# A hybrid attention and RWKV-7 block on one core: the place of VectorE's low parts in the attention stage, and three weight loads that wait for TensorE

## The chip, the core and the metric

The kernel runs on one core of one Trainium2 chip. The metric is device time in microseconds (us), the median of the timed runs. Time of the kernel before: 856.06 us, median of 3 runs (855.99 to 856.78).

## What is computed

One decoder block on 512 tokens of width 1024, all in float32:

```
h = rms_norm(x, attn_norm_g)
u = h @ w_in                                  # 1024 -> 1536 attention + 1792 RWKV + 2048 gates
o_sb = stick_breaking_attention(q, k, v)      # 8 heads of 64, causal
o_rw = rwkv7_time_mix(u_rw, ...)              # 8 heads of 64, a recurrence over the tokens
merged = g_sb * (o_sb @ w_up_sb) + g_rw * (o_rw @ w_up_rw)
x = x + merged @ w_out
x = x + square(relu(rms_norm(x) @ w_ff1)) @ w_ff2
x = x + sigmoid(rms_norm(x) @ w_ple_gate) * (p @ w_ple_proj)
return rms_norm(x, final_norm_g)
```

In stick-breaking attention a weight is `exp(log_sigmoid(z) + reversed running sum of log_sigmoid(-z))` over the scores `z` of a causal row. The change touches the order of the work in the attention stage and in the RWKV stage alone.

## The kernel before, in words

**Split products.** A float32 product is done as three products of rounded parts: both operands are split into a high part (a rounded copy in the format fp32r, made by ScalarE) and a low part (the rest, a subtraction on VectorE). TensorE multiplies high by high, low by high and high by low. For weights this is `mm3` (L244 to L246): w_hi with the high and low parts of the activations, then w_lo. The low part of an operand is thus used last, and always comes out of VectorE.

**Weights.** They come as 512 KB units in the order of the list `seq`. A unit's life is: `load_to` issues the load of `w_raw` on SyncE's queue (L182; four buffers), ScalarE casts it to `w_hi` (L225), VectorE subtracts to get `w_lo` (L227), TensorE uses both. `fetch_to` traces cast and subtraction a few units ahead (`AHEAD = 3`) of the unit that is used. Units are named by kind and number: U_QKV (attention's queries, keys and values), U_RW (RWKV's inputs), U_GSB and U_GRW (the two gates), U_UPSB (attention's up-projection).

**Attention** (about 22 to 145 us). The 8 heads go in pairs (`hp` 0 to 3). While head n is worked on, TensorE's stream is filled with the projections of the next pair and with the first RWKV projections; the function `drive` interleaves generators step by step. For each head there are three blocks. `scores` makes z (L511, L512, into `ps_z`), ScalarE and VectorE make from it `sp` (L519) and split it into `sph` and `spl` (L274, L275). `attend` multiplies `sph` and `spl` by a triangular matrix for the running sums (L558, L562), ScalarE takes the exponential into `sp`, VectorE rounds it to `wh` (L564) and subtracts to get `wl` (L565), and TensorE multiplies `wh` and `wl` by the values into `ps_o` (L550). This line of work, scores to ps_o, is called the chain below. Beside it `projected` splits the next pair's queries (qT, L447, into `qq` and on VectorE `ql`, L455) and keys (kT, L459, into `kk`, whose low half VectorE writes at L463).

**RWKV** (about 150 to 400 us). For each pair `prepare` builds the recurrence's small matrices, `scan` runs the recurrence of the pair before, and `filling` puts gate and up-projections between their steps. In `prepare` the inverse of small triangular matrices is built from 32x32 products: L877 (64 of them to a group), L937 (32), L945 (32); then 64x64 products (L956, 32). The gates' results are written to DRAM by SyncE (L739) and read again later (L725).

**What sets the order.** Each engine runs its own queue in order. A scheduler puts the traced instructions in place on each engine. `tc.issue_after(x)` around an instruction makes it stand behind x on x's engine; it is an order of issue alone and waits for nothing else. `tc.add_manual_dep(a, b, Sync)` makes a really wait until b is done, also across engines.

Of the kernel before, what the change touches and what calls it, by code (L numbers as in the profile page):

```python
# [14 lines left out]
ALU = mybir.AluOpType  # L15
# [78 lines left out]
def tile_block(ctx: ExitStack, tc: tile.TileContext, xT, xt, pT, wts, lora, cols_d, gfin_d, consts_d, out, dbg=None):  # L94
# [65 lines left out]
    ready, loaded, sums12 = {}, [], {}  # L160
    state = {"i": 0, "used": 0, "due": 0}
    AHEAD = 3
    homes = {}
    sources = {}
    sP4 = {}
# [10 lines left out]
    def load_to(n):  # L176
        while len(loaded) < min(n, len(seq)):
            i = len(loaded)
            loaded.append(None)
            if seq[i] not in sources and seq[i][0] not in (U_S3, U_S4):  # L180
                loaded[i] = wpool.tile([P, 1024], F32, name="w_raw", bufs=4)
                sync.dma_start(out=loaded[i], in_=unit(i))  # L182
                if seq[i][0] == U_FF2 and seq[i][2] == 3:
                    pool.dma_start(out=loaded[i], in_=wts[UBASE[U_FF2] + seq[i][1] * 8 + 4 + seq[i][3]], accum_op=ALU.add)

# [10 lines left out]
    def made(i):  # L196
# [10 lines left out]
            return sums12.pop(seq[i][1:])[:, 2]  # L207
        return loaded[i]

    def fetch_to(n, ahead=0):  # L210
        while state["i"] < min(n, len(seq)):
            i = state["i"]
            state["i"] += 1
            load_to(i + 1 + ahead)
            raw = made(i)
            if seq[i] in homes:
                hi, lo = homes[seq[i]]()
            elif seq[i][0] == U_S4:
                hi = wpool.tile([P, 512], F32R, name="w_hi4", bufs=1)
                lo = wpool.tile([P, 512], F32R, name="w_lo4", bufs=1)  # L220
            else:
                hi = wpool.tile([P, 1024], F32R, name="w_hi")
                lo = wpool.tile([P, 1024], F32R, name="w_lo")
            with tc.issue_after(state["hx"] if seq[i] == (U_FF1, 4) else state["fourth"][0]) if seq[i] in ((U_FF1, 4), (U_OUT, 2), (U_OUT, 3)) else nullcontext():
                state["cast"] = act.copy(out=hi, in_=raw).ins  # L225
            with tc.issue_after(state["fourth"][1]) if seq[i] in homes and seq[i][0] == U_OUT else nullcontext():
                state["wlo"] = dve.tensor_tensor(out=lo, in0=raw, in1=r32(hi), op=ALU.subtract).ins  # L227
            if seq[i] == (U_OUT, "s", 4):
                state["fourth"] = state["cast"], state["wlo"]
            ready.setdefault(seq[i], []).append((hi, lo))  # L230
# [99 lines left out]
    with ExitStack() as sA:  # L330
# [43 lines left out]
        with ExitStack() as s1:  # L374
# [68 lines left out]
            def projected(hp, i, ps):  # L443

                if i == 0:
                    t = p1.tile([P, T], F32, name="qT", tag="qkv", bufs=3)
                    dve.scalar_tensor_tensor(out=t, in0=ps, scalar=0.125, in1=rs, op0=ALU.mult, op1=ALU.mult)  # L447

                    qq = [p1.tile([P, T], F32R, name=f"qq{hh}") for hh in range(2)]

                    ql = qls[hp % 2]
                    for hh, (sl, ot) in enumerate((HALVES, HALVES[::-1])):
                        act.copy(out=qq[hh][sl], in_=t[sl])
                        pool.tensor_copy(out=qq[hh][ot], in_=t[sl])
                        dve.tensor_tensor(out=ql[hh][sl], in0=t[sl], in1=r32(qq[hh][sl]), op=ALU.subtract)  # L455
                    heads[hp] = [qq, ql]
                elif i == 1:
                    t = p1.tile([P, T], F32, name="kT", tag="qkv", bufs=3)
                    dve.tensor_tensor(out=t, in0=ps, in1=rs, op=ALU.mult)  # L459
                    kk = [p1.tile([P, T], F32R, name=f"kk{hh}") for hh in range(2)]  # L460
                    for hh, (sl, ot) in enumerate((HALVES, HALVES[::-1])):
                        act.copy(out=kk[hh][sl], in_=t[sl])
                        dve.tensor_tensor(out=kk[hh][ot], in0=t[sl], in1=r32(kk[hh][sl]), op=ALU.subtract)  # L463
                    heads[hp].append(kk)
                else:
                    t = p1.tile([P, T], F32, name="vT", tag="qkv", bufs=3)
                    dve.tensor_tensor(out=t, in0=ps, in1=rs, op=ALU.mult)
                    late.append([3, hp, t])
# [29 lines left out]
            def scores(hp, hh, got):  # L498

                qq, ql, kk = heads[hp][:3]  # L500
                sp = p1.tile([P, 1280], F32, name="sp")
                sph = p1.tile([P, 1280], F32R, name="sph")
                spl = p1.tile([P, 1280], F32R, name="spl")
                zt = {}
                got.update(zt=zt, sp=sp, sph=sph, spl=spl)
                for b, js in BLOCKS:
                    zt[b] = ps_z()

                    for j in js:
                        s = slice(j * P, (j + 1) * P)  # L510
                        pe.matmul(z(zt, j), kk[hh][:, s], qq[hh][:, j * P:T], start=j < 3, stop=False, skip_group_check=True)  # L511
                        pe.matmul(z(zt, j), kk[hh][:, s], ql[hh][:, j * P:T], start=False, stop=False, skip_group_check=True)  # L512
                        pe.matmul(z(zt, j, 0, P), ident_b, caus_b, start=False, stop=True, skip_group_check=True)
                    s, n = BANKS[b]
                    e = sp[:, s:s + n]
                    act.activation(out=e, in_=zt[b][:, :n], func=AF.Abs)
                    act.activation(out=e, in_=e, func=AF.Exp, scale=-1.0)
                    act.activation(out=e, in_=e, func=AF.Ln, bias=1.0)
                    dve.scalar_tensor_tensor(out=e, in0=zt[b][:, :n], scalar=0.0, in1=e, op0=ALU.max, op1=ALU.add)  # L519
                    split(sph[:, s:s + n], spl[:, s:s + n], e)  # L520
                    if b == 1:

                        sums = p1.tile([P, 512], F32, name="sums", bufs=1)
                        hi, lo = (p1.tile([P, 640], F32R, name=name) for name in ("sums_hi", "sums_lo"))
                        for to, i in ((0, 2), (256, 1)):
                            for part, d in ((sph, hi), (spl, lo)):
                                pool.tensor_copy(out=d[:, to:to + P], in_=part[:, ZB[i]:ZB[i] + P])
                        dve.tensor_tensor(out=sums[:, 0:P], in0=sp[:, ZB[2] + P:ZB[2] + 2 * P], in1=sp[:, ZB[3]:ZB[3] + P], op=ALU.add)
                        split(hi[:, P:2 * P], lo[:, P:2 * P], sums[:, 0:P])
                        for c, other in ((0, sp[:, ZB[2]:ZB[2] + P]), (P, sums[:, 0:P])):  # L530
                            dve.tensor_tensor(out=sums[:, 256 + c:384 + c], in0=sp[:, ZB[1] + P + c:ZB[1] + 2 * P + c], in1=other, op=ALU.add)
                        pool.tensor_copy(out=hi[:, 384:640], in_=sums[:, 256:512])
                        pool.tensor_tensor(out=lo[:, 384:640], in0=sums[:, 256:512], in1=r32(hi[:, 384:640]), op=ALU.subtract)
                        got["later"] = hi, lo
                    yield

            def attend(hp, hh, got):
# [17 lines left out]
                for b, js in BLOCKS:  # L555
                    s, n = BANKS[b]
                    for part in (sph, spl):
                        pe.matmul(zt[b][:, :n], tri, part[:, s:s + n], start=False, stop=False, skip_group_check=True)  # L558
                    j = js[0]
                    for part, later in zip((sph, spl), got["later"]):  # L560
                        after = (later[:, 256:640], later[:, 0:256], part[:, ZB[3]:ZB[3] + P])[j]
                        pe.matmul(z(zt, j, P), neg, after, start=False, stop=part is spl, skip_group_check=True)  # L562
                    state["exp"] = act.activation(out=sp[:, s:s + n], in_=zt[b][:, :n], func=AF.Exp)
                    dve.tensor_copy(out=wh[:, s:s + n], in_=sp[:, s:s + n])  # L564
                    dve.tensor_tensor(out=wl[:, s:s + n], in0=sp[:, s:s + n], in1=r32(wh[:, s:s + n]), op=ALU.subtract)  # L565
                    yield
                    output(before)
                    before = js
# [68 lines left out]
        with ExitStack() as s2:  # L637
# [108 lines left out]
            def prepare(hp, got):  # L746
# [187 lines left out]
                ps3 = ps[:, 0:256].rearrange("p (k x) -> p k x", k=8)  # L934
                for k in range(8):
                    for r in (0, 2):
                        pe.matmul(ps3[QUADS[r + 1], k], LM[QUADS[r], k, r // 2, 32:64], X[QUADS[r], k, :], start=True, stop=True)  # L937
                for r in (0, 2):
                    act.copy(out=Yc[QUADS[r + 1]], in_=ps3[QUADS[r + 1]])
                yield  # L940
# [748 lines left out]
```

## Time and profile before

| | |
|---|---|
| median of 3 timed runs | 856.06 us (855.99 to 856.78) |
| the profiled execution | 859.3 us, of it the span 857.5 us and 1.8 us around it |
| mean granted clock of TensorE | 0.996 |
| chain that ended last, by engine | PE 87%, DVE 9%, issue 1%, ACT 1%, DMA 1% |
| DMA over the span | 145 GB/s, 124.23 MB |

PE is TensorE, DVE VectorE, ACT ScalarE, POOL GpSimd, SP SyncE; SPq is SyncE's issuing. A row of the timeline gives start and duration in us, engine, line, operation, result <- operands, tile shape, count, and in brackets the idle time ahead of it with what ended it; "issue" there means that no other engine's work is seen to end the wait. Matmuls are pipelined, so where one instruction waited the spacing of the starts says more than the idle figure. A row of windows gives for a stretch its length, then for PE, PEld (TensorE's weight loads), DVE, ACT and POOL the busy time and number of instructions, then the clock granted to TensorE, the DMA engines' busy share and GB/s. A row of waits gives the total, the count and the longest. A row of the DMA queues gives packets, MB and the share of 16 engines' time.

### The profile page before, as it was taken

How to read it: one execution, taken by the hardware profiler on the slowest of the kernel's cores; microseconds unless marked ns; L12 is line 12 of the kernel's file. 1: busy time of each engine (PE TensorE's matmuls, PEld its weight loads, DVE VectorE, ACT ScalarE, POOL GpSimd, SP SyncE). 2: the span in 40 equal slices, each digit the busy share in tenths (PEclk: the TensorE clock that was granted, in tenths of full speed). 3: DMA queues.
4: the chain of work that ended last, by engine and by line, in shares of the span. 5: the costliest groups of instructions: out<-in, count | busy, mean ns of one | idle time of the engine just before them, and what ended most of it. 6: DMA issues, size and time to landing. Idle time of an engine off the chain costs nothing.

```text
span 857.5 us, 14647 instructions
## 1 busy us (share of the span) xinstructions
PE 840.8 (98%) x5594; PEld 697.5 (81%) x5594; DVE 712.6 (83%) x1264; ACT 513.1 (60%) x804; POOL 105.5 (12%) x174
## 2 busy tenths in 40 slices
PE   8999999999999999999999999999999999999996
PEld 5778788777777777777888888899889989988885
DVE  7989987896987969867896597899879988997767
ACT  7878887734436243533585575458647844783843
POOL 1332432001212101020000101000110010010000
PEclk9999999999999999999999999999999999999999
DMA  8311213421220323427882676973985489275402
GB/s 320 101 50 62 87 62 135 123 96 54 63 88 25 103 83 115 162 97 232 284 258 95 189 228 156 232 202 102 227 234 150 139 240 241 96 221 145 174 23 99
DMA packets 40197, 124.23 MB, mean 145 GB/s; under 512 B 4544, under 2 KB 4544, under 8 KB 40128
## 3 DMA queue, kind: packets, MB, share of 16 engines
q1 hardware_dynamic: 34944, 104.42, 35.7%
q0 software_dynamic: 5184, 18.88, 12.1%
q8 instruction: 44, 0.72, 0.4%
q14 instruction: 25, 0.20, 0.1%
HBM read 108.08 MB, written 10.49 MB: 138 GB/s over the span
## 4 chain that ended last, share of the span: by engine, by line
PE 87%; DVE 9%; issue 1%; ACT 1%; DMA 1%; SPq 0%; DVEq 0%; ACTq 0%
PE ps_m L244 14%; PE ps_m L245 14%; PE ps_m L246 14%; PE ps_m L260 9%; PE ps_m L259 9%; PE ps_m L261 9%; PE ps_g L877 1%; DVE w_lo L227 1%; PE ps_o L550 1%; PE ps_s L1005 1%; PE ps_z L558 1%; PE ps_c L996 1%; PE ps_g L967 1%; DVE LX L899 1%; DVE own L888 1%
## 5 line engine op out<-in xcount | busy, mean ns | idle before, releaser
L225 ACT CAST w_hi<-w_raw 128x1024 fp32r<-128x1024 f32 x122 | 128.0, 1051 | 122.4 <-PE ps_m L245 77.4
L227 DVE TENSOR_TENSOR w_lo<-w_raw,w_hi 128x1024 fp32r<-128x1024 f32 x122 | 149.0, 1224 | 24.2 <-ACT w_hi L225 23.5
L244 PE MATMUL ps_m<-h_hi,w_hi 128*128 128x512 f32 x320 | 130.6, 410 | 0.8 <-ACT w_hi L274 0.7
L246 PE MATMUL ps_m<-h_hi,w_lo 128*128 128x512 f32 x320 | 128.6, 402 | 0.0
L245 PE MATMUL ps_m<-h_lo,w_hi 128*128 128x512 f32 x320 | 128.2, 401 | 0.3 <-DVE h_lo L407 0.3
L244 PEld LDWEIGHTS ps_m<-h_hi,w_hi 128*128 128x128 f32 x320 | 60.7, 190 | 12.6 <-ACT w_hi L274 1.1
L246 PEld LDWEIGHTS ps_m<-h_hi,w_lo 128*128 128x128 f32 x320 | 60.4, 189 | 12.0
L245 PEld LDWEIGHTS ps_m<-h_lo,w_hi 128*128 128x128 f32 x320 | 60.5, 189 | 11.3 <-DVE h_lo L407 1.3
L245 PE MATMUL ps_m<-hx,w_hi 128*128 128x256 f32 (+1 forms) x208 | 65.8, 316 | 0.0
L244 PE MATMUL ps_m<-hx,w_hi 128*128 128x256 f32 (+1 forms) x208 | 65.8, 316 | 0.0
L246 PE MATMUL ps_m<-hx,w_lo 128*128 128x256 f32 (+1 forms) x208 | 65.7, 316 | 0.0
L244 PE MATMUL ps_m<-tb,w_hi 128*128 128x256 f32 x192 | 54.3, 283 | 0.0
L245 PE MATMUL ps_m<-tb,w_hi 128*128 128x256 f32 x192 | 54.3, 283 | 0.0
L246 PE MATMUL ps_m<-tb,w_lo 128*128 128x256 f32 x192 | 54.3, 283 | 0.0
L259 PE MATMUL ps_m<-w_hi,fS 128*128 128x512 f32 x128 | 49.8, 389 | 0.0
L260 PE MATMUL ps_m<-w_lo,fS 128*128 128x512 f32 x128 | 49.8, 389 | 0.0
L261 PE MATMUL ps_m<-w_hi,fS 128*128 128x512 f32 x128 | 49.8, 389 | 0.0
L245 PEld LDWEIGHTS ps_m<-hx,w_hi 128*128 128x128 f32 x208 | 39.6, 191 | 3.0 <-DVE hx L1158 0.4
L244 PEld LDWEIGHTS ps_m<-hx,w_hi 128*128 128x128 f32 x208 | 39.6, 191 | 2.8 <-ACT hx L1157 0.2
L246 PEld LDWEIGHTS ps_m<-hx,w_lo 128*128 128x128 f32 x208 | 39.6, 191 | 2.5
L259 PE MATMUL ps_m<-w_hi,fA 128*128 128x512 f32 x96 | 37.4, 389 | 0.0
L260 PE MATMUL ps_m<-w_lo,fA 128*128 128x512 f32 x96 | 37.4, 389 | 0.0
(425 smaller groups left out, 2147.2 us busy)
## 6 DMA issues: line engine op xcount, KB each, us to landing
w_raw<-in_wts_dram SPq DMA_DIRECT2D x129, 512.0 KB, 4.0
gates<-gg SPq DMA_DIRECT2D x16, 256.0 KB, 2.0
w_raw<-in_wts_dram POOLq DMA_DIRECT2D x8, 512.0 KB, 6.6
x_in<-in_xT_dram SPq DMA_DIRECT2D x8, 256.0 KB, 5.5
gb<-gates SPq DMA_DIRECT2D x8, 256.0 KB, 4.5
tmp<-gates SPq DMA_DIRECT2D x8, 256.0 KB, 2.9
upsb<-tmp SPq DMA_DIRECT2D x8, 256.0 KB, 5.1
ga<-upsb SPq DMA_DIRECT2D x8, 256.0 KB, 6.2
```

Source lines behind the costliest of these rows:

```text
L225: state["cast"] = act.copy(out=hi, in_=raw).ins
L227: state["wlo"] = dve.tensor_tensor(out=lo, in0=raw, in1=r32(hi), op=ALU.subtract).ins
L244: pe.matmul(ps, wh, xh[:, k, t], start=first, stop=False, skip_group_check=skip)
L245: pe.matmul(ps, wh, xl[:, k, t], start=False, stop=False, skip_group_check=skip)
L246: pe.matmul(ps, wl, xh[:, k, t], start=False, stop=last, skip_group_check=skip)
L259: pe.matmul(ps, xh[:, k + j], wh, start=first and j == 0, stop=False, skip_group_check=True)
L260: pe.matmul(ps, xh[:, k + j], wl, start=False, stop=False, skip_group_check=True)
L261: state["row"] = pe.matmul(ps, xl[:, k + j], wh, start=False, stop=last and j == 1, skip_group_check=True).ins
L550: pe.matmul(ps_o[:, j * P:T], vv[:, j, hh, :, :].rearrange("p a d -> p (a d)"), part[:, ZB[j]:ZB[j] + ZN[j]], start=j == 2 and part is wh, ...
L558: pe.matmul(zt[b][:, :n], tri, part[:, s:s + n], start=False, stop=False, skip_group_check=True)
L877: last = pe.matmul(ps[rows, k], left[rows, k, :], rhs[rows, k], start=True, stop=True)
L888: dve.tensor_tensor(out=own8[rows], in0=own, in1=b8[rows].broadcast_to([32, 8, 32]), op=ALU.mult)
```

## The change

It has two parts.

**Attention: low parts behind the chain's.** A variable `state["urgent"]` holds VectorE's latest low part of the chain: the last `spl` that `scores` traced or the last `wl` that `attend` traced. The subtractions for `w_lo` of the U_QKV and U_RW units, for `ql` and for `kk` are traced inside `behind()`, so each of them stands on VectorE behind the chain's latest low part.

**RWKV: three raw loads wait.** The loads of U_GRW units 5 and 6 and of U_UPSB unit 3 wait for the last matmul of the group L937 in `prepare` of pair 2 (both gate units) and of pair 3 (the up-projection unit).

```diff
+    LATER = {(U_GRW, 5): 2, (U_GRW, 6): 2, (U_UPSB, 3): 3}
...
-                sync.dma_start(out=loaded[i], in_=unit(i))
+                load_ = sync.dma_start(out=loaded[i], in_=unit(i))
+                if seq[i] in LATER:
+                    tc.add_manual_dep(load_.ins, state["lm", LATER[seq[i]]].name,
+                                      mybir.DependencyInfo(mybir.DependencyClass.Sync, mybir.DependencyReason.DATA), reason="order")
...
+    def behind():
+        return tc.issue_after(state["urgent"]) if "urgent" in state else nullcontext()
...
-            with tc.issue_after(state["fourth"][1]) if seq[i] in homes and seq[i][0] == U_OUT else nullcontext():
+            with tc.issue_after(state["fourth"][1]) if seq[i] in homes and seq[i][0] == U_OUT else behind() if seq[i][0] in (U_QKV, U_RW) else nullcontext():
                 state["wlo"] = dve.tensor_tensor(out=lo, in0=raw, in1=r32(hi), op=ALU.subtract).ins
...
-                        dve.tensor_tensor(out=ql[hh][sl], in0=t[sl], in1=r32(qq[hh][sl]), op=ALU.subtract)
+                        with behind():
+                            dve.tensor_tensor(out=ql[hh][sl], in0=t[sl], in1=r32(qq[hh][sl]), op=ALU.subtract)
...
-                        dve.tensor_tensor(out=kk[hh][ot], in0=t[sl], in1=r32(kk[hh][sl]), op=ALU.subtract)
+                        with behind():
+                            dve.tensor_tensor(out=kk[hh][ot], in0=t[sl], in1=r32(kk[hh][sl]), op=ALU.subtract)
...
                     split(sph[:, s:s + n], spl[:, s:s + n], e)
+                    state["urgent"] = state["lo"]
...
-                    dve.tensor_tensor(out=wl[:, s:s + n], in0=sp[:, s:s + n], in1=r32(wh[:, s:s + n]), op=ALU.subtract)
+                    state["urgent"] = dve.tensor_tensor(out=wl[:, s:s + n], in0=sp[:, s:s + n], in1=r32(wh[:, s:s + n]), op=ALU.subtract).ins
...
-                        pe.matmul(ps3[QUADS[r + 1], k], LM[QUADS[r], k, r // 2, 32:64], X[QUADS[r], k, :], start=True, stop=True)
+                        state["lm", hp] = pe.matmul(ps3[QUADS[r + 1], k], LM[QUADS[r], k, r // 2, 32:64], X[QUADS[r], k, :],
+                                                    start=True, stop=True).ins
```

The kernel's lines move by 7 to 11 (L227 is L234 after, L455 is L463, L463 is L472, L182 is L183, L739 is L749).

Of the order on VectorE, the place where pair 3's queries are split, before (sp, spl, wh, wl belong to the chain):

```order
L227 TENSOR_TENSOR w_lo<-w_raw,w_hi 128x1024
L275 TENSOR_TENSOR spl<-sp,sph 128x512
L564 CAST wh<-sp 128x256
L455 TENSOR_TENSOR ql_196<-qT,qq_1010 64x512
L565 TENSOR_TENSOR wl<-sp,wh 128x256
L455 TENSOR_TENSOR ql_197<-qT,qq_1011 64x512
```

And after:

```order
L234 TENSOR_TENSOR w_lo<-w_raw,w_hi 128x1024
L582 TENSOR_TENSOR oo<-ps_o,oo 64x512
L528 SCALAR_TENSOR_TENSOR sp<-ps_z,sp 128x512
L454 SCALAR_TENSOR_TENSOR qT<-ps_m,rs 128x512
L282 TENSOR_TENSOR spl<-sp,sph 128x512
L574 CAST wh<-sp 128x256
L575 TENSOR_TENSOR wl<-sp,wh 128x256
L463 TENSOR_TENSOR ql_196<-qT,qq_1010 64x512
L463 TENSOR_TENSOR ql_197<-qT,qq_1011 64x512
```

w_lo has moved up ahead of oo, sp and qT; both ql stand behind wl.

Still on VectorE, the place where pair 3's keys are split, before:

```order
L459 TENSOR_TENSOR kT<-ps_m,rs 128x512
L227 TENSOR_TENSOR w_lo<-w_raw,w_hi 128x1024
L463 TENSOR_TENSOR kk_1121<-kT,kk_1121 64x512
L463 TENSOR_TENSOR kk_1122<-kT,kk_1122 64x512
L519 SCALAR_TENSOR_TENSOR sp<-ps_z,sp 128x512
L572 TENSOR_TENSOR oo<-ps_o,oo 64x512
L564 CAST wh<-sp 128x256
L275 TENSOR_TENSOR spl<-sp,sph 128x512
L565 TENSOR_TENSOR wl<-sp,wh 128x256
```

And after:

```order
L467 TENSOR_TENSOR kT<-ps_m,rs 128x512
L528 SCALAR_TENSOR_TENSOR sp<-ps_z,sp 128x512
L582 TENSOR_TENSOR oo<-ps_o,oo 64x512
L574 CAST wh<-sp 128x256
L282 TENSOR_TENSOR spl<-sp,sph 128x512
L472 TENSOR_TENSOR kk_1121<-kT,kk_1121 64x512
L472 TENSOR_TENSOR kk_1122<-kT,kk_1122 64x512
L234 TENSOR_TENSOR w_lo<-w_raw,w_hi 128x1024
L575 TENSOR_TENSOR wl<-sp,wh 128x256
```

sp, oo, wh and spl now precede the two kk; the two kk and w_lo precede wl, since the low part that they stand behind is spl.

On SyncE's queue, the place where the two gate units are loaded in the RWKV stage, with what each waits for (a semaphore's name, the engine or DMA queue that raises it), before:

```order
L739 DMA gates<-gg 128x512 [waits DVE_49]
L182 DMA w_raw<-in_wts_dram 128x1024 [waits DMAHW2_49,DMAHW0_49,DVE_49]
L739 DMA gates<-gg 128x512 [waits DVE_49]
L182 DMA w_raw<-in_wts_dram 128x1024 [waits DMAHW3_49,DVE_49]
L739 DMA gates<-gg 128x512 [waits DVE_49]
L182 DMA w_raw<-in_wts_dram 128x1024 [waits DMAHW4_49,DVE_49]
```

And after:

```order
L749 DMA gates<-gg 128x512 [waits DVE_49]
L183 DMA w_raw<-in_wts_dram 128x1024 [waits DMAHW2_49,DMAHW0_49,DVE_49]
L749 DMA gates<-gg 128x512 [waits DVE_49] x2
L183 DMA w_raw<-in_wts_dram 128x1024 [waits DMAHW3_49,PE_49,Activation_49]
L183 DMA w_raw<-in_wts_dram 128x1024 [waits DMAHW4_49,DVE_49]
```

The load with `PE_49` is unit 5's; the second write of gates in this place has moved ahead of it, and unit 6's load stands right behind it. At unit 3 of U_UPSB one read of gates (L725) has moved ahead of the waiting load and one stays behind it.

## The prediction

> **What bounds the kernel now.** First the page's totals and its instruction queue.
>
> ```profile
> PE 840.8 (98%) x5594; PEld 697.5 (81%) x5594; DVE 712.6 (83%) x1264; ACT 513.1 (60%) x804; POOL 105.5 (12%) x174
> q8 instruction: 44, 0.72, 0.4%
> ```
>
> TensorE is busy for 98% of the span, so the change can only win what TensorE waits, or works at a lower clock. Queue q8 brought 44 packets, 0.72 MB, so 16 KB each; TensorE has 5594 matmuls and as many weight loads, 11188, and 11188 / 44 = 254 a packet. Then the waits of TensorE over the span (in total, times, longest):
>
> ```profile
> PE ps_g L937 <- issue: 1.4, 1, 1.4
> PE ps_o L550 <- DVE wl L565: 0.8, 2, 0.5
> PE ps_g L877 <- issue: 0.4, 1, 0.4
> PE ps_z L558 <- DVE spl L275: 0.3, 1, 0.3
> ```
>
> These are the waits that the two parts can reach: the first and third in the RWKV stage, where no engine ends them, the others in attention, where VectorE does. Three stretches put sizes to them: attention, the stretch between the two "issue" waits, and the 3.5 us behind the first.
>
> ```profile
> 22.00:145.00 123.00, 121.17 (x609) 98.02 (x608) 108.49 (x193) 98.80 (x181) 36.61 (x62) 1.00 0.23 74
> 306.90:358.81 51.91, 50.45 (x510) 39.14 (x510) 41.63 (x105) 23.63 (x38) 6.57 (x13) 0.97 0.36 118
> 308.70:312.20 3.50, 3.50 (x66) 3.22 (x63) 1.51 (x6) 1.31 (x3) 0.00 (x0) 0.51 0.00 0
> ```
>
> Attention leaves TensorE idle for 123.00 - 121.17 = 1.8 us, with VectorE at 108.49 of 123. [...] And behind the first wait the granted clock was 0.51 for about 3.4 us.
>
> **The RWKV part.** Pair 2 at the first wait, then the same groups in pair 1, where nothing waits:
>
> ```profile
> 305.04 0.50 PE L937 MATMUL ps_g<-LX,LM 32*32 32x32 f32 x20
> 306.92 0.38 PE L937 MATMUL ps_g<-LX,LM 32*32 32x32 f32 x12 [1.37 <-issue]
> 308.55 0.96 PE L945 MATMUL ps_g<-Z,LX 32*32 32x32 f32 x32
> 309.44 1.97 PE L956 MATMUL ps_g<-Vt,LM 64*64 64x64 f32 x32
> 311.34 0.79 PE L244 MATMUL ps_m<-h_hi,w_hi 128*128 128x512 f32 x1
> ```
>
> ```profile
> 252.41 0.69 PE L937 MATMUL ps_g<-LX,LM 32*32 32x32 f32 x32
> 255.53 0.69 PE L945 MATMUL ps_g<-Z,LX 32*32 32x32 f32 x32
> 256.16 1.15 PE L956 MATMUL ps_g<-Vt,LM 64*64 64x64 f32 x32
> 257.24 0.50 PE L244 MATMUL ps_m<-h_hi,w_hi 128*128 128x512 f32 x1
> ```
>
> The group L937 lasts from 305.04 to 307.30, 2.26 against 0.69: the stall costs 1.57. The three groups in the low clock cost 0.96 - 0.69 = 0.27, 1.97 - 1.15 = 0.82 and 0.79 - 0.50 = 0.29, together 1.38. The second "issue" wait, in pair 3, costs 0.4.
>
> [...]
>
> ```profile
> 297.75 0.33 SPq L182 DMA_DIRECT2D w_raw<-in_wts_dram  x1
> 299.91 0.33 SPq L182 DMA_DIRECT2D w_raw<-in_wts_dram  x1
> 353.07 0.33 SPq L182 DMA_DIRECT2D w_raw<-in_wts_dram  x1
> 358.55 2.06 SPq L725 DMA_DIRECT2D tmp<-gates  x2
> ```
>
> ```profile
> q1 hardware_dynamic: 168, 0.56, 47.1%
> ```
>
> ```profile
> q8 instruction: 1, 0.02, 3.7%
> ```
>
> The first two loads are those of gate units 5 and 6. In the 3.1 us after 301.4 the engines moved 0.56 MB of data and no instruction packet; the packet shows only from 304.5 on, when the data is through, and TensorE goes on at 306.92, at most 2.4 us later. To be in time for the 21st product, due at 305.5, it has to start some 1.4 us sooner. The two loads are what filled that time; held until L937 is done they cannot. The load at 353.07 is that of U_UPSB unit 3, ahead of the second wait, and it is treated alike. [...]
>
> What the holds cost: two loads are issued after 305.5 instead of at 297.75 and 299.91, and one about 361 (an estimate: pair 3's L937 is the next step but one behind the L877 whose wait ends at 358.81) instead of at 353.07. Their casts are far behind:
>
> ```profile
> 334.62 1.04 ACT L225 CAST w_hi<-w_raw 128x1024 fp32r<-128x1024 f32 x1 [2.21 <-PE ps_m L245]
> 389.58 1.05 ACT L225 CAST w_hi<-w_raw 128x1024 fp32r<-128x1024 f32 x1 [0.68 <-ACT y L1027]
> ```
>
> 334.62 is unit 5's cast and 389.58 that of U_UPSB 3: 28 us or more of cover, so nothing is paid; without the cover each would cost the delay of 6 to 8 us. On SyncE's queue the gates' write that stood behind unit 5's load now stands ahead, and unit 6's load behind the waiting one is itself held. At U_UPSB 3 the second of the two reads of gates, issued by 360.6 before (358.55 + 2.06), stands behind the load until about 361: it is late by under 1 us, which is also the most that it can cost. I cost these at nothing. [...] Sum: -(1.57 + 1.38 + 0.4) = -3.35.
>
> The clock: the low stretch begins 1.4 us after the gap's end, and the same groups ran at full clock in pair 1, so I let it go with the gap. [...]
>
> **The attention part.** It adds no work; it moves VectorE's subtractions. What it removes is seen where pair 3's queries are split:
>
> ```profile
> 91.57 1.22 DVE L227 TENSOR_TENSOR w_lo<-w_raw,w_hi 128x1024 fp32r<-128x1024 f32 x1
> 92.70 1.10 DVE L275 TENSOR_TENSOR spl<-sp,sph 128x512 fp32r<-128x512 f32 x1
> 93.72 0.70 DVE L564 CAST wh<-sp 128x256 fp32r<-128x256 f32 x1
> 94.34 0.67 DVE L455 TENSOR_TENSOR ql<-qT,qq 64x512 fp32r<-64x512 f32 x1
> 94.94 0.41 DVE L565 TENSOR_TENSOR wl<-sp,wh 128x256 fp32r<-128x256 f32 x1
> ```
>
> ```profile
> 93.80 0.39 PE L246 MATMUL ps_m<-h_hi,w_lo 128*128 128x512 f32 x1
> 94.48 0.39 PE L550 MATMUL ps_o<-wh,vv 128*128 128x256 f32 x1 [0.30 <-DVE wh L564]
> 95.41 0.38 PE L550 MATMUL ps_o<-wl,vv 128*128 128x256 f32 x1 [0.54 <-DVE wl L565]
> 95.63 0.40 PE L558 MATMUL ps_z<-sph,tri 128*128 128x512 f32 x1
> ```
>
> A 512-column matmul takes 0.23 from start to start and a 256-column one half of it (95.63 - 95.41 = 0.22 bounds it above). So 94.48 - 93.80 lost 0.45 and 95.41 - 94.48 lost 0.81, 1.26 where the idle figures show 0.84, a factor of 1.5. After the change w_lo is earlier and ql behind wl, and both waits go. The other two waits of the list, 0.3 each on wl (0.8 - 0.54) and spl, times 1.5 are 0.9. With the small rest, the attention waits that can go are 2.4; the ceiling is the whole idle time, 1.8 x 1.5 = 2.7.
>
> What it adds: whatever stands behind the latest low part *in the trace* may stand ahead of the next one. Replaying the new order by hand gives three places. In pair 2 both ql now come behind spl and ahead of wh and wl, and there was no slack:
>
> ```profile
> 65.56 1.38 DVE L455 TENSOR_TENSOR ql<-qT,qq 64x512 fp32r<-64x512 f32 x2
> 67.91 0.43 DVE L565 TENSOR_TENSOR wl<-sp,wh 128x256 fp32r<-128x256 f32 x1
> 68.39 0.39 PE L550 MATMUL ps_o<-wl,vv 128*128 128x256 f32 x1
> ```
>
> wl ends at 68.34 and is used at 68.39. The 1.38 stand ahead of it in either order, but spl, which moves up, waits for ScalarE's high part, so about 1.0 shows. In pair 3 the keys:
>
> ```profile
> 103.95 1.41 DVE L463 TENSOR_TENSOR kk<-kT,kk 64x512 fp32r<-64x512 f32 x2
> 104.84 0.31 PE L511 MATMUL ps_z<-qq,kk 128*128 128x256 f32 x1
> ```
>
> kk was ready at 104.65 for its first half and used at 104.84. Now sp, oo, wh and spl precede it, which moves it behind 107; the first scores have been moved behind the L558 pair, to about 107.0, and would wait 0.8. And in pair 1 w_lo (1.22) now precedes an spl, which I put at 0.5 on the next wl. Together 2.3: the attention part comes out at 0.1, taken as nothing. Its bounds are -2.7 (all waits go, none comes) and +2.3 (none goes).
>
> **The sum.** Profiled execution: 859.3 - 3.35 = 856.0. The median of the timed runs is 3.24 below the profiled execution; taking the same 3.3 off it gives 856.06 - 3.3 = 852.8. About 0.2% (1.7 us) is what a measurement of this kernel can tell from no change, so "faster" means below 854.35 and "slower" above 857.77.
>
> **Rivals.** (1) As forecast, with attention within 1.5 of nothing: 852.8, between 851.3 and 854.3. For it: the two "issue" waits, a block apart; chance 0.45. (2) The timed runs already lack the first stall: fetch stalls depend on moments, and 3.24 between profile and median is near 1.57 + 1.38 = 2.95, or is the profiler's own price. Then only the 0.4 is left: 855.7. Chance 0.20. (3) The old attention waits go and no new one comes, since VectorE's own slack takes up the moves: 852.8 - 2.4 = 850.4. Against it: 0.05 us of slack at 68.39; chance 0.12. [...] Chance 0.08. [...] Chance 0.05. (6) Slower: low parts of keys and weights stand in front of wl in every later pair. At full price that is 1.41 + 1.22 = 2.6 for each of three pairs, 7.9, less 3.35 and 2.4: +2.1, 858.2. It decides once the new waits pass 3.35 + 2.4 + 1.7 = 7.5; I found 2.3. Chance 0.10.
>
> **How the numbers follow.** Faster: 0.45 + 0.12 + 0.05 = 0.62. Same: 0.20 + 0.08 = 0.28. Slower: 0.10. The range runs from 850.4, the middle of case 3, to 857.0, which takes in cases 2 and 4 with 0.9 to 1.3 of attention's loss; left out are half of case 3 and case 6, 0.16. The likeliest case's own range is 851.3 to 854.3.
>
> **What would show it.** Right: no "issue" wait at L937 or L877, the group L937 of pair 2 at 0.69, the granted clock 1.00 in the 3.5 us behind it, an instruction packet that starts while no load runs, and the casts of the held units where they were. In attention: no waits near 94.5 and 95.4 on the old rows, new ones on wl in pair 2 and on kk in pair 3. Wrong would be: a new "issue" wait in another place, a clock of 0.5 without a gap, a PE wait on `w_hi` of a held unit, or attention's idle time, 1.8 now, above 4.

## The result and the profile after

The changed kernel takes 858.47 us, median of 7 runs (858.11 to 859.48), the kernel before 855.99 in the runs beside it (855.21 to 856.78, 7 runs). The ratio is 1.0034, 95% interval 1.0024 to 1.0044: slower, where faster was forecast. The two profiled executions say something else: 859.12 after (span 857.3 and 1.8 around it) against 859.3 before. Two runs of the experiments below, 2108.98 us (the keys with the queries) and 1659.93 us (the loads done twice), lie far outside all the others: the medians given there count them, the ratios leave them out.

The stages of the profiled execution explain that. The last matmul into ps_o, which ends the attention stage, first before, then after:

```profile
138.88 0.40 PE L550 MATMUL ps_o<-wl,vv 128*128 128x512 f32 x1
```

```profile
142.90 0.40 PE L560 MATMUL ps_o<-wl,vv 128*128 128x512 f32 x1
```

Attention is 4.0 us longer, and the rest of the program 4.2 us shorter (spans of 857.5 and 857.3). The waits of TensorE over the span, after:

```profile
PE ps_z L520 <- DVE kk L472: 2.3, 1, 2.3
...
PE ps_o L560 <- DVE wh L574: 0.9, 1, 0.9
PE ps_o L560 <- DVE wl L575: 0.9, 2, 0.6
...
PE ps_z L572 <- DVE spl L282: 0.6, 1, 0.6
```

No "issue" wait is left in that list, which goes down to 0.2 us, and a wait for the keys' low part, kk, heads the list. The window 22 to 145, attention, after:

```profile
22.00:145.00 123.00, 118.06 (x592) 95.95 (x591) 107.73 (x191) 96.77 (x178) 38.84 (x56) 0.99 0.21 67
```

TensorE is idle there for 123.00 - 118.06 = 4.94 us, where it was 1.8. The RWKV part did in this execution what the prediction read from the profile before. Pair 2's groups after, and the DMA queues in the window 305 to 306:

```profile
308.64 0.69 PE L947 MATMUL ps_g<-LX,LM 32*32 32x32 f32 x32
...
310.60 0.69 PE L956 MATMUL ps_g<-Z,LX 32*32 32x32 f32 x32
311.23 1.15 PE L967 MATMUL ps_g<-Vt,LM 64*64 64x64 f32 x32
312.30 0.50 PE L251 MATMUL ps_m<-h_hi,w_hi 128*128 128x512 f32 x1
```

```profile
q8 instruction: 1, 0.02, 6.6%
```

All four durations are those of the undisturbed pair 1 (0.69, 0.69, 1.15, 0.50), and the instruction packet runs with no data beside it.

The largest part of the loss sits at pair 3's keys. VectorE, ScalarE and TensorE there, after:

```profile
103.49 0.68 DVE L467 TENSOR_TENSOR kT<-ps_m,rs 128x512 f32<-128x512 f32 x1
106.69 0.69 DVE L528 SCALAR_TENSOR_TENSOR sp<-ps_z,sp 128x512 f32<-128x512 f32 x1 [2.52 <-ACT sp L527]
107.30 0.68 DVE L582 TENSOR_TENSOR oo<-ps_o,oo 64x512 f32<-64x512 f32 x1
107.91 0.28 DVE L574 CAST wh<-sp 128x256 fp32r<-128x256 f32 x1
108.21 0.69 DVE L282 TENSOR_TENSOR spl<-sp,sph 128x512 fp32r<-128x512 f32 x1
108.93 1.40 DVE L472 TENSOR_TENSOR kk<-kT,kk 64x512 fp32r<-64x512 f32 x2
```

```profile
104.20 0.62 ACT L470 CAST kk<-kT 64x512 fp32r<-64x512 f32 x1
105.38 0.62 ACT L470 CAST kk<-kT 64x512 fp32r<-64x512 f32 x1
106.02 0.63 ACT L527 ACTIVATE sp<-sp 128x512 f32<-128x512 f32 x1
```

```profile
107.11 0.39 PE L253 MATMUL ps_m<-h_hi,w_lo 128*128 128x512 f32 x1
109.77 0.55 PE L520 MATMUL ps_z<-qq,kk 128*128 128x256 f32 x1 [2.26 <-DVE kk L472]
```

VectorE is idle for 2.52 us up to 106.69. The high parts that the two kk subtractions need are ready at 104.82 and 106.00, when ScalarE's casts end, so as far as its operands go the first of them could have run in that time. But kk has been queued behind spl, spl stands behind sp, and sp waits for ScalarE, which ends its part of sp at 106.65. TensorE starts the next scores 2.66 us after the matmul ahead, 2.43 more than the 0.23 of such a matmul (from its start to the next, as from 106.88 to 107.11). And in this execution the clock falls at the end of the gap: it is 1.00 from 107.50 to 109.40 and 0.50 from 109.45 to 112.80, while TensorE goes on at 109.77. The window 109 to 113:

```profile
109.00:113.00 4.00, 3.23 (x10) 2.71 (x11) 3.62 (x6) 1.22 (x3) 0.00 (x0) 0.57 0.11 13
```

The stretch from these scores to the L572 behind them (112.89) takes 3.12 us here. In the low parts alone, below, where the clock stayed at 1.00, it takes 1.72 (109.09 to 110.81): the low clock costs 1.40.

### The profile page after: what moved, and what is told of

Its sections match the earlier page's. It is cut to its first block, busy times and chain, and to the rows that moved or that the text cites. A ratio compares the mean times of both kernels' runs of the same rounds, so it can differ in the third digit from the quotient of the medians.

```text
span 857.3 us, 14641 instructions
## 1 busy us (share of the span) xinstructions
PE 839.7 (98%) x5594; PEld 697.7 (81%) x5594; DVE 712.8 (83%) x1264; ACT 513.0 (60%) x804; POOL 109.4 (13%) x174
## 4 chain that ended last, share of the span: by engine, by line
PE 85%; DVE 10%; ACT 2%; issue 1%; DMA 1%; SPq 0%; POOL 0%; ACTq 0%; DVEq 0%
PE ps_m L251 14%; PE ps_m L252 14%; PE ps_m L253 14%; PE ps_m L266 9%; PE ps_m L268 9%; PE ps_m L267 9%; PE ps_g L887 1%; DVE w_lo L234 1%; PE ps_o L560 1%; PE ps_s L1016 1%; PE ps_c L1007 1%; DVE LX L909 1%; PE ps_z L568 1%; DVE own L898 1%; PE ps_g L857 1%
## 5 line engine op out<-in xcount | busy, mean ns | idle before, releaser
L232 ACT CAST w_hi<-w_raw 128x1024 fp32r<-128x1024 f32 x122 | 128.0, 1050 | 119.8 <-PE ps_m L252 75.6
L234 DVE TENSOR_TENSOR w_lo<-w_raw,w_hi 128x1024 fp32r<-128x1024 f32 x122 | 149.4, 1228 | 23.8 <-ACT w_hi L232 23.3
```

## The experiments

All medians are of 5 to 12 runs, beside runs of the kernel before on the same chip, whose median was 855.64 in the first group of four, 855.65 in the second and 855.54 in the third. Ratios are to that, with a 95% interval.

### The holds alone

```diff
-            with ... else behind() if seq[i][0] in (U_QKV, U_RW) else nullcontext():
+            with ... else nullcontext():
...
-                        with behind():
-                            dve.tensor_tensor(out=ql...)
+                        dve.tensor_tensor(out=ql...)
```

(and the same for kk.)

> The change's RWKV part alone: the three loads wait, no low part is moved. Theory A (the forecast's): the 1.57 us stall and the 1.38 us of low clock of the profiled execution are in the timed runs too; then 3.3 us faster than before, 852.7. Theory B (rival 2): the timed runs mostly lack them. In the profiles the attention stage became 4.0 us longer and the timed runs 2.5 us, so by B the holds are worth about 1.5: 854.5. Theory C: the holds bring nothing in timed runs: 856.0 within 0.4. In the profile all three expect no issue wait at the group of L937.

Measured: 854.84, ratio 0.999 (0.9982 to 0.9999). That is 0.8 less than before: theory B in kind, with half the price that I gave it. No "issue" wait in the profile. The gain is small beside the noise: its interval reaches from 0.1 to 1.5 us, and the kernel before, run once more in the same group, has a median 0.5 below the 855.64.

### The low parts alone

```diff
-    LATER = {(U_GRW, 5): 2, (U_GRW, 6): 2, (U_UPSB, 3): 3}
+    LATER = {}
```

> The change's attention part alone: low parts behind the chain's, no load waits. With the same bookkeeping as for the holds alone: theory A 858.5 + 3.3 = 861.8; theory B 858.5 + 1.5 = 860.0, 4.0 slower than before, as the attention stage's length in the profile says; theory C 858.5. In the profile the wait for kk in pair 3 (2.3 us) and the low clock behind it as with the whole change.

Measured: 859.32, ratio 1.0038 (1.0026 to 1.005), 3.7 more than before. With the holds' -0.8 that makes +2.9, beside +2.5 for the whole change: the two parts add up within their intervals, which are wide. The five runs fall apart: 857.56 and 857.86 at a mean clock of 0.998, 859.32 to 859.94 at 0.996; 0.002 of 857 us is 1.7 us. So of the 3.7, the runs at 0.998 show 1.9 and 2.2. The two runs of the whole change at 0.998, 858.11 and 858.30, lie 2.1 and 2.3 above the kernel before beside them: at the same clock the holds' gain is not seen between these few runs. Nor do the seven runs of the whole change fall apart so clearly (858.22 at 0.996, 859.48 at 0.997). The profile is of the run at 857.56. The same wait and the same window width there:

```profile
109.09 0.35 PE L520 MATMUL ps_z<-qq,kk 128*128 128x256 f32 x1 [2.26 <-DVE kk L472]
```

```profile
109.00:113.00 4.00, 3.90 (x22) 3.31 (x23) 3.89 (x8) 2.83 (x7) 0.29 (x1) 1.00 0.24 63
```

With an idle time of 2.26 us at the same instruction, the clock of this window is 0.57 in one execution and 1.00 in another.

### The kernel before once more

Nothing is edited.

> The kernel before, unchanged, for another profile and more times. Theory A: its profile again has the issue wait of 1.4 us at L937 and a mean clock of 0.996. Theory B: the wait comes in some executions only: a profile without it, with the RWKV stage 1.5 to 3 us shorter, or runs that differ by about 3 us. The time itself: 856.0 by both.

Measured: 855.14, ratio 0.9999 (0.999 to 1.0008), one of the 12 runs at 859.19 with a clock of 0.993; its profiled execution took 856.23. The group L937 of pair 2 in it:

```profile
304.59 0.50 PE L937 MATMUL ps_g<-LX,LM 32*32 32x32 f32 x20
305.71 0.38 PE L937 MATMUL ps_g<-LX,LM 32*32 32x32 f32 x12 [0.62 <-issue]
...
307.38 0.69 PE L945 MATMUL ps_g<-Z,LX 32*32 32x32 f32 x32
```

The wait is at the same product, but 0.62 instead of 1.37, and L945 behind it takes 0.69, and the clock from 150 to 395 is 1.00: no low stretch there. The group takes 305.71 + 0.38 - 304.59 = 1.50, 0.81 over 0.69, close to the 0.80 that the holds alone gained. But this execution, too, lies 1.09 above the median of its runs, so a usual run may have less of the stall. Of 35 runs of the kernel before beside the second group, 33 lie between 854.64 and 856.50 and two at 858.41 and 858.52, with a clock of 0.996 where the others have 0.997 to 0.999. The execution on which the forecast was made, 859.3 at 0.996, is of that kind; the other two groups have one such run each, of 29 and of 27.

### The raw loads done twice

To see whether the raw loads' data are what the instructions wait for, the kernel before loads units 5 and 6 of U_GRW twice.

```diff
                 sync.dma_start(out=loaded[i], in_=unit(i))
+                if seq[i] in ((U_GRW, 5), (U_GRW, 6)):
+                    sync.dma_start(out=loaded[i], in_=unit(i))
```

> The kernel before, with the raw loads of gate units 5 and 6 done twice, the second right behind the first (same data, same place), so that the DMA queues are busy some 3 to 6 us longer where TensorE's next block of instructions is fetched. Theory: the block waits behind the loads' data; the issue wait at L937 grows to 2 us or more in every execution, with the low clock behind it, and the median goes up by 2 to 5 us: 858 to 861. Rival: the wait has to do with something else, or the fetch shares the queues: 855.6, no issue wait above 0.6.

Measured: 856.24, ratio 1.0007 (0.9998 to 1.0016). The time is not told from before. The issue wait is 0.45 in the profile: neither number of the theory came, and the rival's "no issue wait above 0.6" did. The DMA queues in the window 303 to 304, first of this kernel, then of the kernel before once more:

```profile
q1 hardware_dynamic: 53, 0.17, 90.1%
q8 instruction: 1, 0.02, 5.8%
```

```profile
q1 hardware_dynamic: 13, 0.02, 6.4%
q8 instruction: 1, 0.02, 5.5%
```

And in the window 301 to 302, of the holds alone:

```profile
q8 instruction: 1, 0.02, 8.8%
```

With the loads in front the packet shows two windows later than without them, which I read as a delay by the loads. But here it did not wait until the data were through: with the second pair of loads, issued from 301.65 on, it is in the same window as with the first pair alone, amid data at 90.1%. That is a reading of three windows of one execution each, not a test of the queue.

### The low parts without the keys

```diff
-                        with behind():
-                            dve.tensor_tensor(out=kk...)
+                        dve.tensor_tensor(out=kk...)
```

and LATER is empty.

> The attention part alone without the keys: w_lo and ql stay behind the chain's low part, kk's subtraction is where it was. Theory K (the keys carry the loss: 2.43 us of wait in pair 3, 1.36 of low clock behind it): 3.8 less than the attention part with keys, about 856.2 by theory B, no different from before. Rival W (any low part that is pushed behind spl comes ahead of the next wh or wl, so ql in pair 2 with 1.1 and w_lo take their share, and the keys' slot is taken by w_lo): 858 or more.

Measured: 856.46, ratio 1.0006 (0.9997 to 1.0015): theory K's time. The keys account for 859.32 - 856.46 = 2.9 of 3.7, the low clock included: all runs here have 0.997 to 0.999, and over them the two runs at 0.998 with the keys lie 1.1 and 1.4. Rival W has its places in the profile all the same (0.7 on wh in pair 2, 1.2 on wl in pair 3), in part paid for by the waits near 94 that are gone.

### Each kind alone

In all three LATER is empty, and `behind()` stands around one of the three subtractions only: w_lo, kk, ql.

> The attention part for w_lo alone; ql and kk are where they were, no load waits. Theory: each of the three kinds pays by itself, by what it is put in front of. In the profile of the part without the keys the wl of pair 3 waits 1.40 us behind a w_lo, and the early spl 0.4 more than before; so w_lo alone costs 1.4 to 1.8 us: 857.0 to 857.5, with a wait on wl near 107. Rival: the places come about only by the three kinds together (the keys' move leaves the slot that w_lo takes): 855.6 within 0.4.

Measured: 855.58, ratio 0.9997 (0.9989 to 1.0006). The wait is where the theory has it, behind a w_lo (VectorE, then TensorE):

```profile
106.41 1.22 DVE L234 TENSOR_TENSOR w_lo<-w_raw,w_hi 128x1024 fp32r<-128x1024 f32 x1
107.55 0.42 DVE L573 TENSOR_TENSOR wl<-sp,wh 128x256 fp32r<-128x256 f32 x1
```

```profile
108.02 0.38 PE L558 MATMUL ps_o<-wl,vv 128*128 128x256 f32 x1 [1.10 <-DVE wl L573]
```

but the time is the rival's: the waits near 94 that go (1.26, of which 0.28 is left) pay for most of it.

> The attention part for the keys' low parts alone; w_lo and ql are where they were, no load waits. Theory: the keys carry the loss: TensorE waits 2.4 us for kk in pair 3, and in the executions in which the clock drops behind it 1.4 to 2 more: 858.0 to 859.5. Rival: the wait needs w_lo moved as well: 856.5 or less.

Measured: 856.73, ratio 1.0012 (1.0002 to 1.0021), 1.1 more than before. Between the two: slower, but by less than the theory's 2.4. VectorE's wait ahead of sp is 0.95, and TensorE's for kk 0.86 (1.02 by the starts):

```profile
103.89 0.69 DVE L527 SCALAR_TENSOR_TENSOR sp<-ps_z,sp 128x512 f32<-128x512 f32 x1 [0.95 <-ACT sp L526]
...
106.13 1.40 DVE L471 TENSOR_TENSOR kk<-kT,kk 64x512 fp32r<-64x512 f32 x2
```

```profile
106.96 0.35 PE L519 MATMUL ps_z<-qq,kk 128*128 128x256 f32 x1 [0.86 <-DVE kk L471]
```

> The attention part for the queries' low parts alone; w_lo and kk are where they were, no load waits. Theory: it takes away the pair of waits in pair 3 (1.26 us) and adds one of 0.85 to 1.1 ahead of wh in pair 2: 855.3, the same as before. Rival: without w_lo moved ahead the gain isn't there, and the loss is: 856.7.

Measured: 855.66, ratio 1.0001 (0.9992 to 1.0009), the theory's time by another sum: the pair of waits near 94 is not gone but 1.01 instead of 1.26, and a wait of 0.5 for kk has come at 104.

Alone the three cost -0.1, 1.1 and 0.0, together 3.7, or 1.9 and 2.2 in the runs at 0.998.

### The keys with one other kind

LATER is empty; `behind()` stands around kk and ql, and around kk and w_lo.

> Keys' and queries' low parts behind the chain's, w_lo where it was, no load waits. With the keys alone TensorE waits 1.0 us for kk in pair 3, with all three kinds 2.4, since there VectorE's sp of the block before came 1.4 us late. Theory Q: the queries' move makes that sp late; then the wait for kk is 2 us or more here, and the time 858 or more. Rival: w_lo's move does it; then kk's wait is 1.0 to 1.3 as with the keys alone and the time 856.5 to 857.

Measured: 857.06, ratio 1.0014 (1.0005 to 1.0023), 1.5 more than before; the wait for kk is 1.5 us. The interval overlaps that of the keys alone.

> Keys' low parts and w_lo behind the chain's, ql where it was, no load waits. Theory Q: kk's wait stays near 1.0 us, and the time is 856.5 to 857. Rival (w_lo's move makes the sp before late): kk's wait is 2 us or more and the time 858 or more.

Measured: 858.35, ratio 1.0034 (1.0021 to 1.0046), 2.8 more than before; the wait for kk is 1.7 us. The rival of theory Q comes nearest, with a wait below the 2 us that it asked for: w_lo does most of it and ql a part. VectorE in this kernel:

```profile
102.72 0.68 DVE L466 TENSOR_TENSOR kT<-ps_m,rs 128x512 f32<-128x512 f32 x1
105.92 0.69 DVE L527 SCALAR_TENSOR_TENSOR sp<-ps_z,sp 128x512 f32<-128x512 f32 x1 [2.52 <-ACT sp L526]
```

With w_lo out of the place between kT and sp, VectorE has nothing to do there: the same 2.52 us of idle time as in the whole change, which w_lo and kk used to fill (1.64 and 1.41 in the profile before).

The idle time alone does not make the wait grow. In the four kernels that move the keys, sp starts 3.19 to 3.20 us behind kT and kk 2.24 to 2.25 behind sp, with w_lo between kT and sp or without it. What differs is how early VectorE starts the sp of the block before, which stands ahead of kT. Here it is, with the scores that TensorE computes meanwhile, for the keys alone and for the whole change:

```profile
98.38 0.69 DVE L527 SCALAR_TENSOR_TENSOR sp<-ps_z,sp 128x512 f32<-128x512 f32 x1 [0.29 <-ACT sp L526]
99.57 0.39 PE L519 MATMUL ps_z<-qq,kk 128*128 128x512 f32 x1
```

```profile
101.19 0.68 DVE L528 SCALAR_TENSOR_TENSOR sp<-ps_z,sp 128x512 f32<-128x512 f32 x1
100.97 0.39 PE L520 MATMUL ps_z<-qq,kk 128*128 128x512 f32 x1
```

| moved | start of this sp ahead of these scores, us | wait for kk by the starts, us |
|---|---|---|
| kk | 1.19 | 1.02 |
| kk, ql | 0.60 | 1.62 |
| kk, w_lo | 0.39 | 1.83 |
| all three | -0.22 | 2.43 |

The sum of the two columns is 2.21 to 2.22 in each row. So the keys' own move costs a wait of about 1.0; moving ql as well makes VectorE reach this sp 0.59 later, moving w_lo 0.80 and both 1.41 (in the kernel with kk and w_lo, w_lo runs from 98.02 to 99.33, ahead of wh, wl and this sp). TensorE waits for kk that much longer.

### Two attempts at a version that keeps the gain

Both have the holds. One puts `behind()` around ql of pair 3 alone, the other around the w_lo of one unit alone.

```diff
-                        with behind():
+                        with behind() if hp == 3 else nullcontext():
```

> The holds and of the attention part one place alone: pair 3's queries' low parts stand behind the chain's. wl then follows wh at once, so of the two waits there the one on wl (0.81 us) goes and nothing else moves on VectorE: 0.8 below the holds alone, 854.0, 1.6 below before. Rival: the time comes back at the next wait on VectorE, since ql is due in the next scores: 854.8.

Measured: 855.14, ratio 0.9996 (0.9987 to 1.0004).

```diff
-            ... else behind() if seq[i][0] in (U_QKV, U_RW) else nullcontext():
+            ... else behind() if seq[i] == (U_RW, 12) else nullcontext():
```

> The holds, and of the attention part one instruction alone: the w_lo of unit 12 of U_RW, which stood ahead of spl, wh and wl where pair 3's queries are split (1.22 us), stands behind them. Theory: the two waits there (0.45 and 0.81) go and nothing else moves; 0.9 to 1.2 below the holds alone: 853.7. Rival: the time is given back at the next wait for VectorE, as it was when the queries alone were moved there (0.5 us on kk): 854.6.

Measured: 854.95, ratio 0.9994 (0.9985 to 1.0003). In both the rival holds: nothing below the holds alone (854.84). The waits near 94 shrink, and TensorE then waits for VectorE at the next keys, in the first kernel for 0.4 us, in the second for 0.9:

```profile
PE ps_z L518 <- DVE kk L470: 0.9, 1, 0.9
PE ps_o L558 <- DVE wl L573: 0.5, 2, 0.3
```

The holds alone have the lowest median of the kernels run. They are clearly faster than the changed kernel, and by an interval that just leaves out no change faster than the kernel before; these two attempts can't be told from them.

## Why the prediction was wrong, point by point

**"Profiled execution: 859.3 - 3.35 = 856.0 ... taking the same 3.3 off" the median: failed.** With the holds the stall and its low clock are gone, as forecast (no "issue" wait in the profiles of the whole change, the holds alone and the one w_lo with the holds, and a clock of 1.00 from 310 to 315 in the first); but the size was that of one execution, and other profiles without the holds list no "issue" wait either: the low parts alone, those without the keys, and the keys with ql (with w_lo there is one of 0.9). Of the 3.35, the 1.57 of the stall is 0.81 in another execution of the same kernel, and the 1.38 of low clock is absent there; the holds alone are worth 0.8 in timed runs. This is rival 2, which said 855.7 for attention at nothing, where 854.84 was measured, and which I gave 0.20. The sign was to be read on record: the profiled execution lay 3.24 above the median, and 1.57 + 1.38 is 2.95 of that. A term that explains why an execution is unusual can't be taken off the usual one.

**"What the holds cost": right.** No "issue" wait is in the changed kernel's list of waits, and none for a held unit's high part (L232); unit 5's cast is at 335.20, where it was at 334.62.

**"it has to start some 1.4 us sooner ... held until L937 is done they cannot" fill that time: right.** The packet is in the window 301 to 302 with the holds and 303 to 304 without. That it comes "when the data is through" is refuted by the doubled loads, in the one execution profiled. That the two waits lie "a block apart", the ground of case 1, no run shows: 1020 instructions lie between them, the 254 a packet are a mean over 44 packets, and no row says with which instruction a packet begins. What the runs show is a wait at L937 in some profiles with the loads not held (1.37, 0.62, 0.45 and 0.9 us) and none in others.

**The clock, "I let it go with the gap": right as far as the traces show**, in that both low stretches come with a gap, at a clock of 0.50: before from 308.75 to 312.15, 1.8 us after the end of the gap of 1.37 (not 1.4, as the prediction has it), after from 109.45 to 112.80, from 0.3 us ahead of the end of the gap of 2.26. But a gap doesn't always bring one: the window 109 to 113 has 0.57 and 1.00 with the same 2.26 us, and behind the 0.62 us of the kernel before once more L945 took its 0.69.

**"The attention part comes out at 0.1, taken as nothing": failed**, by 3.7 in the medians and by 1.9 and 2.2 in the two runs at a clock of 0.998. What goes was put at 2.4: the 1.26 near 94 went, but the waits near 41 and 48 (0.9 by my sum) stayed, as the list of waits after shows with spl and wl. What comes was put at 2.3, at the right three places. Pair 2's 1.0 and pair 1's 0.5 were near (1.1 and 0.8 by the starts). Pair 3's keys were put at 0.8, which is near the 1.02 of the keys moved alone; in the whole change they cost 2.43, and 1.40 more where the clock fell. The step that failed is the pricing of the moves one by one: the prediction has no term for the chain's sp, which VectorE reaches 1.41 later when w_lo and ql have moved too, and kk, queued behind the next sp, inherits that. The prediction's own sign of being wrong, attention's idle time above 4, came with 4.94.

**Rival 6, slower: its time, 858.2, is close to the 858.47, but not by its mechanism; the nearness is luck.** It had low parts stand in front of wl at every pair at full price; what decided is one place, where the keys' low part stands behind a chain that waits. The bound of +2.3 on attention lies above the 1.9 and 2.2 only because the 1.26 near 94 went: the waits that came are 1.1 + 0.8 + 2.43 = 4.3 by the starts.

**Shown and open.** Shown: that the attention part loses and the holds do not, the keys' lead in the loss, and how their wait grows with w_lo and ql (1.02 to 2.43). Not separated: how much of the 3.7 in the medians is the low clock, since only some executions have it; why it comes in some is open. The holds' gain is known only to lie between 0.1 and 1.5. A version that defers the w_lo ahead of pair 3's keys too wasn't tried.

## What to carry to other kernels

Before a wait in one profiled execution is priced, hold that execution's time against the median: if it lies above by about the wait's size (here 3.24, beside 1.57 + 1.38), the wait may be what made it unusual. An order of issue, "behind x", can cost more than it buys when x itself waits for another engine: what is put behind x on an in-order queue inherits x's wait, and the idle time ahead of x, which the moved work used to fill, is lost: here VectorE's 2.52 us ahead of sp, where w_lo and kk used to take 1.64 and 1.41. Moves on one queue can't be priced one by one, since what one of them delays, the next one waits for: the wait for kk is 1.02 with the keys moved alone and 2.43 with all three. The cure for one wait of a busy helper engine (VectorE, 108.49 of 123.00 us of attention) can show up at its next one, as the 0.4 and 0.9 us at the next keys did in the two attempts, so a place is only won if the engine's queue up to the next wait is replayed with its waits.

## What the hardware showed that I had not expected

With the same idle time of TensorE, 2.26 us at the same instruction, the granted clock from 109 to 113 is 0.57 in one execution and 1.00 in another; the low clock costs 1.40 us there, and the runs of the low parts alone split by about 2 us along their mean clock (0.998 and 0.996). A packet of the instruction queue showed two windows of 1 us later with loads issued ahead of it (303 to 304 instead of 301 to 302), and no later still with more loads issued from 301.65 on, while the data queue was 90.1% busy; each is seen in one execution.
